# Reordering the first two groups of the MLP's up product, its passage to the down product, and the last norm

## The chip, the cores and the metric

One NeuronCore of a Trainium2 chip runs the whole program; the other seven are idle. The metric is the device time of one execution in microseconds, the median of three runs. The engines are named as in the profile: PE is TensorE (matrix products), PEld its weight loads, DVE is VectorE, ACT is ScalarE, POOL is GpSimd, SP is SyncE, which issues most DMAs. Each engine works through its own list of instructions in order; semaphores tie the lists together.

## The reference, cut to what matters

The network has two layers. Each has a norm, an attention with four groups of heads, and a squared-ReLU MLP; a norm over the result ends it. The change touches the MLP of both layers and the last norm.

```python
def rms_norm(x, g):
    xf = x.astype(jnp.float32)
    y = xf * lax.rsqrt(jnp.mean(xf * xf, axis=-1, keepdims=True) + EPS)
    return (y * g.astype(jnp.float32)).astype(x.dtype)
...
        x = x + mix @ w_out[l]
        h = rms_norm(x, norm2_g[l])
        x = x + jnp.square(jax.nn.relu(h @ w_up[l])) @ w_down[l]
    return rms_norm(x, final_norm_g)
```

There are 1024 tokens of width 1024, the MLP is 4096 wide, and all is float32.

## The kernel before

**Layout.** The activations lie transposed: eight tiles `self.x[m]` of 128 features by 1024 tokens. A float32 product is made of three passes (L219, L220, L221): an operand is split into a rounded part `hi` and a remainder `lo`, and hi·hi, hi·lo and lo·hi are added up in PSUM. A split (`split`, L187 and L193) is one ACT instruction for `hi` and one subtraction for `lo`; for weights (`weight_parts`) the subtraction is on POOL, for activations on DVE. One `block` is the product of a 512x128 piece of weights with 512 tokens: 12 PE instructions of 512 columns.

**The up product** (`mlp_up`) treats weights and activations as 2x2 blocks and makes seven products per group instead of eight. A group `q` of 16 is 128 features of each half of the MLP's width. Its seven blocks are `p12`, `p11`, `p6`, `p5`, `p7`, `p4`, `p3`. They use sums and differences of the four weight pieces (`combos`, tiles `raw`) and seven operands `ops[1]` to `ops[7]`, which are made once per layer out of `x` (tiles `oph`/`opl`, `far`, with the intermediates `t` and `v`). PSUM has two banks each for `u`, `p`, `q`, `mm`. `p11`, `p6`, `p7` and `p4` of one group run into the same bank `u`, and between them ACT copies the state out (L1237, L1247, L1256). The results meet on DVE: the copy of `p7` plus `p5` gives `s.u3` (the addition in `done4`), `p3` and the copy of `p6` give `s.u2`.

The norm is not applied to the operands. Its factor is found beside the products (`sums`, tile `acc`; `rstd_cols`, L266 on PE, L268, L246 to L256) and spread over the partitions by PE (`spread_here`, L302) into `self.rb`. It is multiplied in when a result passes the ReLU (`relu2`, L1220, followed by the square on ACT, L1222). So the first results wait for `rb`. The groups 0 and 1 (`first`) run side by side product by product, because their operands are being made meanwhile; from group 2 on a group runs on its own and the p4 and p3 of the group before come in its middle.

**The passage.** The results go to DRAM (`acts`, L1226) and come back as operands `act` of the down product, which is split into `far` tiles again. `mlp_down` uses the same seven products, in four rounds `j`; all eight PSUM banks are its own. The loads and splits of its first round are called early (high priority, offset `AHEAD`).

**What sets the order.** In the MLP, PE runs in the order in which the code is written (`manual_schedule`). The other engines' lists are laid out by a scheduler that simulates the program and takes the earliest ready instruction. After that every list is fixed. Buffers come from pools: ten `raw` pieces, nine `ev` pieces, three pairs of split weights `wh`/`wl` (a split for a block can start when the block three places before it is done), sixteen wide tiles that hold `far`, `acc`, `t`, `v`.

**The last norm.** `final(n)` works on 512 of the 1024 tokens: for each of eight tiles a square (L1455) and a scaling (L1456) on ACT and an addition on DVE, then `rstd_cols`, a spread on PE, a copy to `self.rb` on DVE (L1465), and per tile one product on DVE and one store. `final(0)` stands ahead of the last four blocks of the down product, `final(1)` behind them.

## Time and profile before

| what | us |
|---|---|
| median of three runs | 2698.26 (2697.42 to 2702.37) |
| the profiled execution | 2701.14 |
| its span, first to last instruction | 2698.9 |
| attention of layer 1 and of layer 2 | 6.8 to 697.9, 1343.4 to 2031.3 |
| up product, layer 1 and 2, begin | 698, 2031 |
| down product, layer 1 and 2, begin | 1037, 2369 |
| PE idle, gaps over 0.2 us in the timeline added up, 640 to 800 | 14.1 |
| the same, 1960 to 2698.9 | 26.8 |

Rows of a timeline give the start, the duration, engine, line, operation, and what is written from what; in brackets stands the idle time of that engine just before and who ended it. Rows of windows give for a stretch its length, the busy time of each engine with the number of instructions (x), the granted clock of TensorE as a share, the share of the DMA engines and their GB/s. PE instructions overlap: one of 512 columns is shown with 0.39 us and more, and the next one starts 0.23 us after it.

### The profile page before, as it was taken

Reading aid. Unit: us, or ns where it says so; the run is one execution under the profiler, and the core shown is the slowest. Engines: PE = TensorE matmul, PEld = TensorE weight load, DVE = VectorE, ACT = ScalarE, POOL = GpSimd, SP = SyncE. Lnnn points to the kernel's source line nnn. Section 1 sums busy time; section 2 is a strip of 40 time slices with the busy share of each in tenths; the row PEclk is TensorE's granted clock in tenths of the full one; section 3 lists DMA queues with packets and bytes.
Section 4 is the critical chain, followed back from the end, with each engine's and each line's share of the span. In section 5 each row is a group of like instructions: output and inputs, shape, how many; then the busy total and the mean of one; then the engine's idle time right before and its main releaser. Section 6 shows DMA issues by size and latency. Waiting matters only on the chain.

```text
span 2698.9 us, 37585 instructions
## 1 busy us (share of the span) xinstructions
PE 2545.4 (94%) x12296; PEld 2109.5 (78%) x12296; DVE 1944.6 (72%) x3368; ACT 1438.1 (53%) x2591; POOL 1151.6 (43%) x816
## 2 busy tenths in 40 slices
PE   8999988999889999999999999789998999999997
PEld 6778876787778887888877788677886788778886
DVE  6777767784966669887568776577749666687776
ACT  4677756663534444444437776566635344444444
POOL 2555633301345554544425655332013455545552
PEclk9989998999999999999999899899999999999998
DMA  5534597421144457444245436963221444664431
GB/s 171 174 94 141 151 268 245 106 89 57 53 140 153 150 166 269 149 139 142 100 128 149 119 114 192 273 199 89 71 71 55 156 150 151 230 219 150 131 102 63
DMA packets 191666, 389.18 MB, mean 144 GB/s; under 512 B 23840, under 2 KB 33008, under 8 KB 191472
## 3 DMA queue, kind: packets, MB, share of 16 engines
q1 hardware_dynamic: 177648, 361.62, 43.3%
q10 hardware_dynamic: 13824, 25.17, 2.7%
q8 instruction: 97, 1.59, 0.2%
q14 instruction: 97, 0.79, 0.1%
HBM read 263.29 MB, written 123.41 MB: 143 GB/s over the span
## 4 chain that ended last, share of the span: by engine, by line
PE 73%; DVE 13%; DMA 5%; ACT 5%; issue 3%; POOL 1%; SPq 0%; DVEq 0%; ACTq 0%; POOLq 0%
PE u L219 8%; PE u L221 8%; PE u L220 8%; PE mm L219 6%; PE mm L220 5%; PE mm L221 5%; PE p L219 5%; PE p L220 5%; PE p L221 5%; PE sb L815 3%; DVE p L817 2%; DVE part L187 2%; PE tr L851 2%; ACT p L820 2%; DVE ptl L187 1%
## 5 line engine op out<-in xcount | busy, mean ns | idle before, releaser
L187 POOL TENSOR_TENSOR wl<-raw,wh 128x512 fp32r<-128x512 f32 x448 | 636.0, 1420 | 699.0 <-ACT wh L193 680.1
L193 ACT ACTIVATE wh<-raw 128x512 fp32r<-128x512 f32 x448 | 281.6, 629 | 575.0 <-PE u L220 314.6
L187 POOL TENSOR_TENSOR wl<-ws,wh 128x512 fp32r<-128x512 f32 (+1 forms) x120 | 151.2, 1262 | 431.2 <-ACT wh L193 427.1
L219 PE MATMUL u<-far,wh 128*128 128x512 f32 x768 | 301.5, 393 | 12.6 <-ACT ev L1247 8.3
L187 DVE TENSOR_TENSOR ptl<-tr,pth 128x512 fp32r<-128x512 f32 (+2 forms) x384 | 239.2, 629 | 88.4 <-ACT pth L193 87.2
L221 PE MATMUL u<-far,wl 128*128 128x512 f32 x768 | 300.8, 392 | 0.8 <-POOL wl L187 0.8
L187 DVE TENSOR_TENSOR raw<-raw 128x512 f32<-128x512 f32 x256 | 222.7, 875 | 107.9 <-POOL wl L187 54.2
L220 PE MATMUL u<-far,wh 128*128 128x512 f32 x768 | 300.5, 391 | 0.0
L193 ACT ACTIVATE pth<-tr 128x512 fp32r<-128x512 f32 (+2 forms) x384 | 206.2, 547 | 123.1 <-PE tr L851 67.2
L820 ACT ACTIVATE p<-p,nm 128x1024 f32<-128x1024 f32 x192 | 220.2, 1147 | 77.3 <-DVE nm L817 72.8
L219 PE MATMUL p<-far,wh 128*128 128x512 f32 x640 | 252.3, 394 | 7.5 <-DVE ev L187 7.5
L221 PE MATMUL p<-far,wl 128*128 128x512 f32 x640 | 251.0, 392 | 1.5 <-POOL wl L187 1.5
L220 PE MATMUL p<-far,wh 128*128 128x512 f32 x640 | 251.2, 392 | 0.0
L815 PE MATMUL sb<-stack 96*128 96x512 f32 x640 | 217.6, 422 | 13.1 <-DVE nm L817 12.8
L187 DVE TENSOR_TENSOR far<-act,far 128x512 fp32r<-128x512 f32 x224 | 210.4, 969 | 14.6 <-ACT far L193 14.6
L187 POOL TENSOR_TENSOR p<-p 128x1024 f32<-128x1024 f32 x64 | 153.5, 2402 | 110.8 <-ACT p L903 103.0
L219 PEld LDWEIGHTS u<-far,wh 128*128 128x128 f32 x768 | 145.4, 189 | 45.2 <-ACT ev L1247 9.2
L851 PE MATMUL tr<-ident,p 128*128 128x128 f32 x1024 | 163.2, 278 | 8.8 <-DVE ptl L187 6.0
L221 PEld LDWEIGHTS u<-far,wl 128*128 128x128 f32 x768 | 145.1, 189 | 32.2 <-POOL wl L187 1.6
L219 PE MATMUL mm<-xh,wh 128*128 128x512 f32 x416 | 168.3, 405 | 1.4 <-DVE part L187 1.2
L220 PEld LDWEIGHTS u<-far,wh 128*128 128x128 f32 x768 | 145.3, 189 | 30.1
L220 PE MATMUL mm<-xl,wh 128*128 128x512 f32 x416 | 165.3, 397 | 0.0
(248 smaller groups left out, 6110.1 us busy)
## 6 DMA issues: line engine op xcount, KB each, us to landing
act<-acts SPq DMA_DIRECT2D x224, 256.0 KB
raw<-in_w_up SPq DMA_DIRECT2D x128, 256.0 KB
acts<-ev SPq DMA_DIRECT2D x128, 256.0 KB
raw<-in_w_down SPq DMA_DIRECT2D x128, 256.0 KB
acts<-ev ACTq DMA_DIRECT2D x96, 256.0 KB
ws<-in_w_in SPq DMA_DIRECT2D x76, 256.0 KB
rz<-drows SPq DMA_DIRECT2D x40, 256.0 KB
stack<-kd SPq DMA_DIRECT2D x32, 256.0 KB
```

The lines of the kernel that those rows point to most:

```text
L187: (eng or self.nc.vector).tensor_tensor(out=out, in0=a, in1=b, op=op)
L193: nc.scalar.activation(hi, src, AF.Copy)
L219: mm(ps, w[0], x[0][:, sl], start=start, stop=False)
L220: mm(ps, w[0], x[1][:, sl], start=False, stop=False)
L221: mm(ps, w[1], x[0][:, sl], start=False, stop=stop)
L815: self.nc.tensor.matmul(ps, q[:, qt * P:(qt + 1) * P], k[:, sl], start=i == 0, stop=i == len(passes) - 1)
L817: self.nc.vector.tensor_tensor_reduce(out=p[:, sl], in0=ps, in1=self.zero[:, 0:1].bitcast(F).broadcast_to([P, 512]), scale=-scale, scalar= ...
L820: self.nc.scalar.activation(p, p, AF.Exp, bias=nm[:, 1:2], scale=-1.0, accum_out=z)
L851: nc.tensor.transpose(t[:, k * 256 + i * P:k * 256 + (i + 1) * P], p[:, (j * 2 + k) * P:(j * 2 + k + 1) * P], self.ident)
```

## The change

It has four parts.

1. The `lo` parts of the weights of groups 0 and 1 (12 per layer) are made on DVE instead of POOL (`self.lows`).
2. At the norm's sum: the addition of `s.u3` moves from `done4` into `p4`, ahead of its block; `p4` of both first groups stands ahead of `rstd_cols`; `p12` of group 2 stands between `rstd_cols` and `spread_here`; and the rest of groups 0, 1 and 2 is interleaved instead of in sequence.
3. At the passage the first splits (`lo` on DVE), products and loads of the down product are queued on DVE behind the last group's addition `s.sum` (`issue_after`).
4. The last norm works on pieces of 512, 256 and 256 tokens, as three generators which are advanced between the last products. The last two weight blocks are split once and multiplied in halves of 256 tokens (`products`, `tail`). The spread factor is read from PSUM by DVE and from a copy of it by POOL, which makes every third of the output products.

```diff
     def weight_parts(self, raw):
...
-        self.split(wh, wl, raw, eng=self.nc.gpsimd)
+        self.split(wh, wl, raw, eng=self.lows)
...
             def p4(s):
+                s.sum = self.tt(s.u3, s.p, s.u3, ALU.add)
                 self.block(s.u, s.c["22"], ops[4], start=False)
...
                 keep(s.q, 2, s.b21)
-                self.tt(s.u3, s.p, s.u3, ALU.add)
                 relu2(s.u3, s.u3, 1)
...
                 first = [group(q) for q in range(2)]
+            self.lows = nc.vector
...
             acc = sums(1, (4, 5, 6, 7, 0, 1, 2, 3), acc)
-            p4(first[0])
+            for s in first:
+                p4(s)
             r = self.rstd_cols(acc, DM, self.ones[:, 0:1])
-            p4(first[1])
+            self.lows = nc.gpsimd
+            s = group(2)
+            p12(s)
             self.spread_here(rb, r)
-            for s in first:
-                done11(s)
-                done4(s)
+            done11(first[0])
+            done4(first[0])
             ops[3] = [self.rows_split(far(), x(k + 4, 1), gk(k + 4)) for k in range(4)]
-            for s in first:
-                p3(s)
-            held = []
-            for q in range(2, 16):
+            p3(first[0])
+            p11(s)
+            done11(first[1])
+            done4(first[1])
+            combos(s.c)
+            p3(first[1])
+            done11(s)
+            p6(s)
+            p5(s)
+            p7(s)
+            held = s
+            for q in range(3, 16):
...
+            self.settled = s.sum
...
-                b = [self.rows_split(self.far(), v) for v in t]
-                for m in M:
-                    self.block(u[m], a11[m], b)
-                    add(m, 0, u[m])
-                a12, b = [w(m, 1, "b") for m in M], op(2)
+                with ExitStack() as behind:
+                    if j == 0:
+                        behind.enter_context(tc.issue_after(self.settled.ins))
+                    b = [self.rows_split(self.far(), v) for v in t]
+                    for m in M:
+                        self.block(u[m], a11[m], b)
+                        add(m, 0, u[m])
+                    a12, b = [w(m, 1, "b") for m in M], op(2)
...
-                if last and j == 3:
-                    self.final(0)
-                for m in M:
+                if not (last and j == 3):
+                    for m in M:
+                        self.block(p[m], a12[m], b, start=False)
+                        add(m, 1, p[m])
+                    continue
+                fin = [self.final(slice(i * 256, i * 256 + w)) for i, w in ((0, 512), (2, 256), (3, 256))]
+                for f in fin:
+                    for m in (4, 5, 6, 7):
+                        next(f)
+                    if f is fin[0]:
+                        for m in M:
+                            next(f)
+                def tail(m, ws, i, f):
+                    sl = slice(i * 256, i * 256 + 256)
+                    self.products(p[m][:, sl], ws, [(h[:, sl], v[:, sl]) for h, v in b])
+                    o = self.x[m][:, 512 + i * 256:512 + i * 256 + 256]
+                    self.tt(o, p[m][:, sl], o, ALU.add)
+                    next(f)
+
+                for m in (0, 1):
                     self.block(p[m], a12[m], b, start=False)
                     add(m, 1, p[m])
-            if last:
-                self.final(1)
+                    for f in fin[1:]:
+                        next(f)
+                    if m == 0:
+                        next(fin[0])
+                ws = [self.weight_parts(a12[m]) for m in (2, 3)]
+                tail(2, ws[0], 0, fin[1])
+                next(fin[0], None)
+                tail(3, ws[1], 0, fin[1])
+                tail(2, ws[0], 1, fin[2])
+                with tc.high_priority(offset=40):
+                    next(fin[1])
+                tail(3, ws[1], 1, fin[2])
...
+        near = self.piece("ev")[:, :w]
+        nc.scalar.activation(near, rb, AF.Copy)
+        yield
+        for i, (m, x) in enumerate(xs):
+            if i % 3 == 1:
+                self.tt(x, x, near, eng=nc.gpsimd)
+            else:
+                self.tt(x, rb, x)
             self.store(self.out[m][:, sl], x)
```

**How the lists stand now: first groups.** A piece of the difference of DVE's list in layer 1, where the operands of groups 0 and 1 are made (`x_7177` and its like are tiles of `x`, `t` an intermediate, `wl` the `lo` part of a weight piece).

```order
 L187 TENSOR_TENSOR acc<-acc,sq 128x512
+L187 TENSOR_TENSOR wl<-raw,wh 128x512
 L187 TENSOR_TENSOR t<-x_7177 128x512
 L187 TENSOR_TENSOR x_7184<-mm,sum 128x512
+L187 TENSOR_TENSOR wl<-raw,wh 128x512
 L187 TENSOR_TENSOR t<-x_7184 128x512
 L187 TENSOR_TENSOR x_7191<-mm,sum 128x512
+L187 TENSOR_TENSOR wl<-raw,wh 128x512
 L187 TENSOR_TENSOR t<-x_7191 128x512
```

The first three of the twelve `wl` have come into DVE's list, between the instructions that make the operands.

**The passage, DVE, before.** The rows from the last of group 14's four differences on; `act` are loaded operands of the down product, `ev_10074<-p_10057,ev_10074` is the addition that becomes `s.sum` of group 15, the `raw` rows are sums and differences of weights for the down product.

```order
L187 TENSOR_TENSOR ev_10030<-ev_10001,ev_10029 128x512
L187 TENSOR_TENSOR far_10170<-act_10162,far_10170 128x512
L187 TENSOR_TENSOR far_10173<-act_10164,far_10173 128x512
L187 TENSOR_TENSOR far_10176<-act_10166,far_10176 128x512
L187 TENSOR_TENSOR raw_10312<-raw_10278,raw_10280 128x512
L187 TENSOR_TENSOR far_10179<-act_10168,far_10179 128x512
L187 TENSOR_TENSOR far_10266<-act_10258,far_10266 128x512
L187 TENSOR_TENSOR raw_10278<-raw_10154,raw_10278 128x512
L187 TENSOR_TENSOR far_10269<-act_10260,far_10269 128x512
L187 TENSOR_TENSOR far_10272<-act_10262,far_10272 128x512
L187 TENSOR_TENSOR raw_10334<-raw_10282,raw_10284 128x512
L187 TENSOR_TENSOR ev_10074<-p_10057,ev_10074 128x512
```

And the same place of the change:

```order
L187 TENSOR_TENSOR ev_10030<-ev_10002,ev_10029 128x512
L187 TENSOR_TENSOR raw_10312<-raw_10278,raw_10280 128x512
L187 TENSOR_TENSOR raw_10278<-raw_10154,raw_10278 128x512
L187 TENSOR_TENSOR raw_10334<-raw_10282,raw_10284 128x512
L187 TENSOR_TENSOR ev_10074<-p_10057,ev_10074 128x512
L187 TENSOR_TENSOR far_10170<-act_10162,far_10170 128x512
L187 TENSOR_TENSOR far_10173<-act_10164,far_10173 128x512
L187 TENSOR_TENSOR far_10176<-act_10166,far_10176 128x512
```

Seven splits have moved from ahead of the addition to behind it; the three `raw` rows stay ahead of it.

**The passage, ACT, before.** A little later in layer 1: `wh_10233` and `wh_10295` are the `hi` parts of the weights of the down product's fourth and fifth block, and the square of `ev_10039` (L1222) waits for DVE's `relu2` of group 15's `s.u2`.

```order
L193 ACTIVATE far_10481<-act_10472 128x512
L1222 ACTIVATE ev_10039<-ev_10039 128x512
L193 ACTIVATE far_10484<-act_10474 128x512
L193 ACTIVATE wh_10233<-raw_10160 128x512
L193 ACTIVATE far_10487<-act_10476 128x512
L193 ACTIVATE wh_10295<-raw_10250 128x512
```

And of the change:

```order
L193 ACTIVATE far_10484<-act_10474 128x512
L193 ACTIVATE far_10487<-act_10476 128x512
L1222 ACTIVATE ev_10039<-ev_10039 128x512
L193 ACTIVATE wh_10233<-raw_10160 128x512
L193 ACTIVATE wh_10295<-raw_10250 128x512
```

The two splits of `act` have moved ahead of the square, and the fourth block's `hi` part stands directly behind it, as before behind the square. The attention of layer 2, which the diff does not touch, also stands in another order on all engines, since the scheduler arrives there in another state; that of layer 1 is unchanged.

More of the change, by code (lines that the diff above doesn't have):

```diff
@@ L147, in __init__ @@
         self.ctx, self.tc, self.nc, self.d, self.out = ctx, tc, tc.nc, d, out
-        self.ahead, self.tails = 4, deque()
+        self.ahead, self.tails, self.lows = 4, deque(), tc.nc.gpsimd
         pool = lambda **k: ctx.enter_context(tc.tile_pool(**k))
@@ L1453, in final @@
             x = self.x[m][:, sl]
[L1454 removed]
+            s = self.piece("ev")[:, :w]
             nc.scalar.activation(s, x, AF.Square)
@@ L1461, in final @@
             xs.append((m, x))
+            yield
         r = self.rstd_cols(acc, DM, self.ones[:, 0:1], "u")
-        rb = self.bank("u")
-        self.spread_half(rb, r, 0)
-        nc.vector.tensor_copy(self.rb[:, sl], rb)
-        for m, x in xs:
-            self.tt(x, x, self.rb[:, sl])
+        yield
+        rb = self.bank("u")[:, :w]
+        for t in range(w // P):
+            nc.tensor.matmul(rb[:, t * P:(t + 1) * P], r[:, t:t + 1].broadcast_to([P, P]), self.ident,
+                             start=True, stop=True)
+        near = self.piece("ev")[:, :w]
+        nc.scalar.activation(near, rb, AF.Copy)
+        yield
+        for i, (m, x) in enumerate(xs):
[3 more added lines that the diff above has]
+                self.tt(x, rb, x)
             self.store(self.out[m][:, sl], x)
```

25 lines of the change are left out of this document (16 added, 9 removed).

## The prediction, made before the change was run

> **What bounds the kernel now.** I read the page's busy shares first, then the windows by stage, then PE's timeline for its gaps, then the list of the engine that ends each gap.
>
> ```profile
> span 2698.9 us, 37585 instructions
> PE 2545.4 (94%) x12296; PEld 2109.5 (78%) x12296; DVE 1944.6 (72%) x3368; ACT 1438.1 (53%) x2591; POOL 1151.6 (43%) x816
> ```
>
> PE is busy 94% of the span, so a gain can only come from PE's idle time and from its halved clock. The windows say where these are.
>
> ```profile
> 6.80:697.90 691.10, 646.69 (x3412) 539.50 (x3413) 491.12 (x1090) 428.34 (x799) 261.26 (x184) 0.96 0.49 146
> 697.95:772.84 74.89, 60.99 (x249) 48.17 (x248) 64.89 (x85) 37.50 (x67) 25.71 (x17) 0.91 0.28 92
> 800.00:850.00 50.00, 50.00 (x221) 41.20 (x220) 34.11 (x40) 21.33 (x38) 25.94 (x18) 1.00 0.45 149
> 1018.30:1041.00 22.70, 17.86 (x70) 13.91 (x69) 22.66 (x29) 12.46 (x23) 7.81 (x6) 0.92 0.88 332
> 1041.00:1071.20 30.20, 28.83 (x126) 23.21 (x126) 30.20 (x36) 15.97 (x27) 18.35 (x12) 1.00 0.54 176
> 1343.40:2031.30 687.90, 641.25 (x3414) 538.16 (x3413) 488.85 (x1081) 423.38 (x793) 258.08 (x183) 0.96 0.47 140
> 2031.27:2105.21 73.94, 60.99 (x250) 47.88 (x248) 65.13 (x85) 37.85 (x67) 25.68 (x17) 0.91 0.29 93
> 2079.00:2086.00 7.00, 6.41 (x29) 5.58 (x30) 5.48 (x10) 1.38 (x3) 0.31 (x1) 0.76 0.20 75
> ```
>
> In the steady up product (800 to 850) PE never waits: 221 instructions in 50 us, 0.226 us each, so a block of 12 costs 2.71 us. The two stretches of 74 and 75 us are the first groups of each layer, up to where group 2 begins its p7. They hold 18 blocks (48.8 us) and 32 short instructions of sum and spread, by my estimate 3.6 us at full clock; the other 22.5 and 21.5 us are waiting and half clock. At the passage (1018 to 1071) DVE is busy without a hole, 22.66 of 22.70 and 30.20 of 30.20 us: DVE, not PE, sets the pace there. PE's gaps:
>
> ```profile
> 728.26 0.50 PE L219 MATMUL u<-far,wh 128*128 128x512 f32 x1 [4.14 <-ACT ev L1247]
> 746.12 0.38 PE L302 MATMUL mm<-ident,rs_r 128*128 128x128 f32 x1 [3.26 <-DVE rs_r L256]
> 764.54 0.80 PE L219 MATMUL u<-oph,wh 128*128 128x512 f32 x1 [3.84 <-ACT ev L1237]
> 1032.25 0.50 PE L219 MATMUL p<-far,wh 128*128 128x512 f32 x1 [3.75 <-DVE ev L187]
> 1045.85 0.50 PE L221 MATMUL u<-far,wl 128*128 128x512 f32 x1 [0.34 <-POOL wl L187]
> 1071.23 0.47 PE L219 MATMUL u<-far,wh 128*128 128x512 f32 x1 [1.06 <-ACT far L193]
> 2079.59 2.48 PE L302 MATMUL mm<-ident,rs_r 128*128 128x128 f32 x16 [2.29 <-DVE rs_r L256]
> 2684.69 0.49 PE L266 MATMUL u<-ones,ev 128*128 128x1 f32 x3 [2.70 <-DVE ev L187]
> ```
>
> A gap costs more than its length. Around the 2.29 us gap at 2079.59 the granted clock over 7 us is 0.76, so 0.24 x 7.00 x 2 = 3.4 us ran at half speed, and 1.7 us of work were lost. I take 1.7 us per new gap of 2 us and more, as this row has it.
>
> **The first groups: lows on DVE.** What a POOL low costs DVE stands in these rows.
>
> ```profile
> 712.25 0.67 DVE L187 TENSOR_TENSOR opl<-t,oph 128x512 fp32r<-128x512 f32 x1
> 712.94 1.73 POOL L187 TENSOR_TENSOR wl<-raw,wh 128x512 fp32r<-128x512 f32 x1 [3.09 <-DVE opl L187]
> 713.46 1.76 DVE L1292 SCALAR_TENSOR_TENSOR t<-x,par,t 128x512 f32<-128x512 f32 x1
> 715.14 0.68 DVE L187 TENSOR_TENSOR far<-v,far 128x512 fp32r<-128x512 f32 x1
> 715.74 0.74 DVE L1292 SCALAR_TENSOR_TENSOR v<-x,par,v 128x512 f32<-128x512 f32 x1
> L187 POOL TENSOR_TENSOR wl<-raw,wh 128x512 fp32r<-128x512 f32 x12 | 17.6, 1473 | 45.1 <-ACT wh L193 40.2 <-DVE opl L187 3.1 <-DVE v L1292 1.8
> ```
>
> The DVE instruction that meets a POOL low takes 1.76 instead of 0.74 us: 1.02 to 1.07 us of DVE per low. On DVE itself a low should cost 0.60 us (0.68 less the overlap with the next, as the starts 715.14 and 715.74 show). So 12 lows moved save DVE 12 x (1.05 - 0.60) = 5 us, and each arrives within 0.7 us instead of 1.47. Bounds: no relief at all, 12 x 0.60 = 7.2 us more on DVE; or every one relieved, and none late.
>
> I followed DVE's new list by count, 0.60 us an addition and 0.66 us a three-operand one, from the end of this addition without its stretch (691.2):
>
> ```profile
> 690.60 1.76 DVE L187 TENSOR_TENSOR acc<-acc,sq 128x512 f32<-128x512 f32 x1
> 695.43 0.69 DVE L187 TENSOR_TENSOR x<-mm,sum 128x512 f32<-128x512 f32 x1 [1.14 <-PE mm L221]
> 737.13 1.47 DVE L187 TENSOR_TENSOR acc<-acc,sq 128x512 f32<-128x512 f32 x2
> 742.63 0.15 DVE L268 TENSOR_SCALAR ms<-mm 128x8 f32<-128x8 f32 x1
> 743.97 1.22 DVE L254 SCALAR_TENSOR_TENSOR rs_t<-rs_r 128x8 f32<-128x8 f32 x1
> 745.90 0.17 DVE L256 SCALAR_TENSOR_TENSOR rs_r<-rs_t,rs_r 128x8 f32<-128x8 f32 x1
> ```
>
> The low of p5 of group 0 is the 32nd instruction (26 x 0.60 + 6 x 0.66 + about 1.2 of waiting for PE, as at 695.43): 712.0. PE wants it at 697.95 + 4 x 2.71 + 0.6 + 2 x 0.226 = 709.9, so PE waits 2.2 us there, 0.6 at p11, and 1.0 at p7 for the last `far<-v`. PE is through both p4 at 697.95 + 12 x 2.71 + 3.8 = 734.3. The sum's last addition is the 68th (56 x 0.60 + 12 x 0.66 + 1.2, and three POOL lows of later blocks, 3.2): 737.1, against 738.6 now. So PE waits for the sum instead, about 2.8 us less 0.9 for the half that is ready. So DVE stays the bound of this stretch; the gain is that p4 of group 1 is done ahead of the sum.
>
> **The norm's sum.** From the last addition: 0.9 us of sum on PE, two operand lows on DVE (1.3), then the chain from `ms` to `rs_r`, 746.07 - 742.63 = 3.44 us now with a stretched step of 1.22, about 3.1 then. The spread starts at 737.1 + 0.9 + 0.5 + 3.2 = 741.7 instead of 746.12, 4.4 us earlier, and p12 of group 2 (2.71) has run under the wait: PE is 7.1 us ahead. The wait of 3.84 us ahead of p6 of group 2, whose copy stands behind eight differences, shrinks to about 1.1, since three differences and one group's squares stand ahead of it now: 9.8 us. The clock at half after 764.54 goes too (about 2.5); against it I book a wait of 2 us at p7 of group 2 (its copy is behind the second group's late squares) and one new half clock, 1.7. Layer 1: **8.6 us**. Layer 2 loses 1 us less now (73.94 against 74.89): **7.6 us**. Bounds for each: 3 (no relief on DVE) to 14 (only the waits that the order forces).
>
> By the Trainium skill (TensorE: Matmul & The Clock Gate, Part 1: The HAM clock gate) half clock follows an idle window of about 3.4 us, so waits of 2 us would cost no clock. The trace shows otherwise (2.29 us, clock 0.76). By the page the sum would be 3.4 us better.
>
> **The passage.** The order shows the addition ahead of seven splits, so the 3.75 us wait at 1032.25 goes and p3 follows p4. What is late next?
>
> ```profile
> 1031.52 0.68 DVE L187 TENSOR_TENSOR ev<-p,ev 128x512 f32<-128x512 f32 x1
> 1040.35 0.68 DVE L1220 SCALAR_TENSOR_TENSOR ev<-ev,rb 128x512 f32<-128x512 f32 x1
> 1041.07 0.63 ACT L1222 ACTIVATE ev<-ev 128x512 f32<-128x512 f32 x1
> 1042.13 0.62 ACT L193 ACTIVATE wh<-raw 128x512 fp32r<-128x512 f32 x1
> ```
>
> The `hi` part of the down product's fourth block (1042.13) stands on ACT behind the square of group 15's `u2` (1041.07), and this behind DVE's `relu2` at 1040.35. In the new list 27 DVE instructions stand between group 14's last difference and that `relu2`, 24 before: it ends about 1.8 us later, at 1042.9, and the fourth block's weights are ready at 1046, as now (1045.85). PE, ahead by 5 us after p3, waits there instead, in one piece, and loses a clock window. DVE's work up to the addition that frees the bank for 1071.23 is the same 58 instructions. So the 3.75 us are not won: I book **-1.5 us** per layer (1.7 of clock, some of it in the 1.06 us of slack). Bounds: +6.5 (3.75, its half clock 1.7 and 1.06 all go) to -3.4 (two windows). If DVE's cover were gone, that is if it had free time here, the upper bound would hold.
>
> **The last norm.**
>
> ```profile
> 2665.56 1.35 POOL L187 TENSOR_TENSOR wl<-raw,wh 128x512 fp32r<-128x512 f32 x1 [0.32 <-ACT wh L193]
> 2665.71 0.68 DVE L187 TENSOR_TENSOR x<-p,x 128x512 f32<-128x512 f32 x1
> 2690.29 4.90 DVE L187 TENSOR_TENSOR x<-x,rb 128x512 f32<-128x512 f32 x8
> 2672.11 23.45 SPq L162 DMA_DIRECT2D out<-x  x16
> ```
>
> Now 34 us pass from the end of the p5 blocks (2664.9) to 2698.9. Then: two blocks and the sum (6.3) to 2671.2, a half block, the spread and a half block (3.7) to 2674.9. Five output products of 0.65 us stand on DVE ahead of the next additions: 2678.5; square, addition and sum: 2679.2; the last half block to 2680.5; addition, square, addition, sum, five products of the middle piece and the chain of `rs_r`: 2685.3; spread, copy and five narrow products: 2687.7. Its stores land 3.7 us later, as now (2690.29 + 4.90 = 2695.2, span end 2698.9): 2691.4, a gain of **7.5 us**. Bounds: 11 (DVE never in the way) to 4 (clock halved in the half blocks, POOL's products last).
>
> The DVE products read PSUM; such a row beside a POOL low keeps its 0.68 us (2665.71), so I charge POOL's nine products nothing. The Trainium skill (SBUF — State Buffer, Who interferes with whom) says this too: only a DVE instruction with two SBUF inputs meets POOL's reads. Charged like the others, they would take 9 x 1.05 = 9.5 us off, and the gain of this part would be gone.
>
> **The second attention** gets another order. The same work takes 691.10 and 687.90 us in two orders now; I take 0, with -5 to +5.
>
> **Sum.** 8.6 + 7.6 - 3.0 + 7.5 = 20.7 us. The profiled execution (span 2698.9, 2701.14 in all) would become 2680.4; it lies 2.9 us above the median, and from the median 2698.26 comes 2677.6. I say **2677 us**.
>
> **Rivals.**
> - *The passage pays.* If DVE is quicker there than my count, each layer wins 6.5 instead of -1.5: 16 us more, 2661. For it: the addition is ahead of the splits. Against: DVE's two full windows. 0.22.
> - *No relief on DVE in the first groups*: 3 us a layer instead of 8, 2687. For it: DVE is full there already. Against: the 0.67 beside the 1.76. 0.15.
> - *Slower.* A low on DVE costs the stretched 1.75 us instead of 0.60, with ACT and PE at the same tiles: 12 x 1.15 = 13.8 us more per layer on DVE, 27.6, and 2705. It decides from about 1.5 us per low. Against it: nothing of POOL runs there any more. 0.05.
> - *No change.* The parts work but the second attention's new order takes them back: 20 of 688 us, 3%. 0.06.
>
> My forecast holds with 0.52 (2668 to 2686). A measurement of this kernel tells 0.2%, 5.4 us, from no change. Faster: 0.52 + 0.22 + 0.15 = 0.89; same 0.06; slower 0.05. The range 2657 to 2690 takes in both faster rivals and leaves out about 0.15.
>
> **What would show it.** In the new trace: no DVE instruction of 1.7 us between 692 and 730; the spread of layer 1 at 741 to 743; p3 of group 15 directly behind p4, then a wait of 4 to 7 us in the fourth block of the down product, ended by ACT `wh` or POOL `wl` at about 1046 less what is won ahead; the last PE instruction about 2685 on the old scale. I am wrong if the fourth block does not wait, or if lows on DVE take over 1 us.

## The result and the profile after

The changed kernel takes **2683.99 us** (median of five runs, 2680.68 to 2689.33), against 2702.37 us (2697.42 to 2707.92) for the kernel before on the same chip: a ratio of 0.9935, 95% interval 0.9915 to 0.9955. Timed once more beside other kernels it took 2684.57 us, ratio 0.9954 (0.9936 to 0.9972). So it is faster by about half a per cent, 12 to 18 us. The prediction said 2677 us, 20.7 us less than before by its sum; the two profiled executions differ by 14.2 us (spans of 2698.9 and 2684.7).

The head of the page of the changed kernel:

```profile
span 2684.7 us, 37657 instructions
PE 2545.3 (95%) x12320; PEld 2113.1 (79%) x12320; DVE 1932.0 (72%) x3402; ACT 1443.0 (54%) x2612; POOL 1121.1 (42%) x801
```

PE is busy as long as before (2545.3 against 2545.4 us): nothing was taken from its work, only from its idle time. The windows of the changed kernel, first groups of both layers, the steady up product, DVE's passage, and the norm's sum with p12 of group 2:

```profile
697.70:766.95 69.25, 60.65 (x250) 48.72 (x248) 61.32 (x93) 37.73 (x67) 11.56 (x8) 0.90 0.29 92
2024.91:2093.80 68.89, 59.99 (x250) 48.12 (x249) 61.23 (x93) 37.85 (x67) 11.44 (x8) 0.90 0.30 98
800.00:850.00 50.00, 50.00 (x221) 41.24 (x220) 34.07 (x40) 20.72 (x37) 26.52 (x19) 1.00 0.46 152
1020.88:1052.00 31.12, 25.22 (x96) 19.73 (x95) 31.12 (x42) 13.31 (x23) 12.05 (x7) 0.89 0.71 249
738.97:745.60 6.63, 6.63 (x21) 5.47 (x22) 4.29 (x10) 1.99 (x5) 0.00 (x0) 0.54 0.00 0
```

The first groups, 74.89 and 73.94 us before, take 69.25 and 68.89. In the fourth row DVE still works without a hole, 31.12 of 31.12 us. The last row is a price: PE runs at 0.54 of its clock over the sum and p12 of group 2. PE's gaps in the timeline of the changed kernel:

```profile
711.93 0.56 PE L221 MATMUL p<-far,wl 128*128 128x512 f32 x1 [1.94 <-DVE wl L187]
738.97 1.37 PE L266 MATMUL mm<-ones,acc 128*128 128x1 f32 x8 [2.33 <-DVE acc L187]
759.72 0.56 PE L219 MATMUL u<-oph,wh 128*128 128x512 f32 x1 [3.67 <-ACT ev L1237]
1031.73 0.47 PE L219 MATMUL u<-far,wh 128*128 128x512 f32 x1 [3.69 <-DVE ev L1220]
1041.79 0.50 PE L221 MATMUL u<-far,wl 128*128 128x512 f32 x1 [2.22 <-POOL wl L187]
2668.15 1.01 PE L266 MATMUL u<-ones,ev 128*128 128x1 f32 x4 [2.22 <-DVE ev L187]
2676.25 1.19 PE L1519 MATMUL u<-ident,rs_r 128*128 128x128 f32 x4 [1.82 <-DVE rs_r L256]
```

Gone are the 4.14 us ahead of p4 of group 0 and the 3.26 us ahead of the spread. Still there is the wait ahead of p6 of group 2 (3.67, 3.84 before). At the passage the 3.75 us ahead of p3 of group 15 are gone, and 3.69 us stand ahead of the second block of the down product.

For a balance I cut both executions at the same pieces of work, by the start times in PE's timeline: first groups (p12 of group 0 to p12 of group 3), steady groups (to p6 of group 15), passage (to the sixth operand's round), rest of the down product (to the next attention; in layer 2 to the end of the fourth operand's round), last norm.

| stretch, us | before | after | after, second profile |
|---|---|---|---|
| attention 1 / 2 | 698.0 / 687.9 | 697.7 / 685.3 | 695.0 / 688.1 |
| first groups, layer 1 / 2 | 77.6 / 76.7 | 72.0 / 71.6 | 70.4 / 71.8 |
| steady groups, each layer | 240.4 | 240.4 | 240.4 |
| passage, layer 1 / 2 | 43.2 / 43.1 | 46.6 / 45.2 | 46.6 / 45.0 |
| rest of the down product, 1 / 2 | 284.2 / 262.5 | 282.9 / 261.1 | 282.9 / 261.1 |
| last norm | 45.0 | 41.5 | 41.2 |

After less before: -0.3 and -2.6 for the attentions, -5.6 and -5.1 for the first groups, +2.1 and +0.8 for passage and rest together, -3.5 for the last norm: -14.2 us, the difference of the spans.

### The profile page after: what moved, and what is told of

It is laid out like the page before. It is cut to its first block, busy times and chain, and to the rows that moved or that the text cites. A ratio compares the mean times of both kernels' runs of the same rounds, so it can differ in the third digit from the quotient of the medians.

```text
span 2684.7 us, 37657 instructions
## 1 busy us (share of the span) xinstructions
PE 2545.3 (95%) x12320; PEld 2113.1 (79%) x12320; DVE 1932.0 (72%) x3402; ACT 1443.0 (54%) x2612; POOL 1121.1 (42%) x801
## 4 chain that ended last, share of the span: by engine, by line
PE 72%; DVE 12%; DMA 6%; ACT 5%; issue 3%; POOL 1%; SPq 0%; POOLq 0%; DVEq 0%; ACTq 0%
PE u L219 8%; PE u L221 8%; PE u L220 8%; PE mm L219 6%; PE mm L220 5%; PE mm L221 5%; PE p L221 5%; PE p L219 5%; PE p L220 5%; PE sb L815 3%; DVE p L817 3%; PE tr L851 2%; DVE part L187 2%; ACT p L820 2%; DVE ptl L187 2%
## 5 line engine op out<-in xcount | busy, mean ns | idle before, releaser
L187 POOL TENSOR_TENSOR wl<-raw,wh 128x512 fp32r<-128x512 f32 x424 | 596.9, 1408 | 725.2 <-ACT wh L193 566.7
L820 ACT ACTIVATE p<-p,nm 128x1024 f32<-128x1024 f32 x192 | 220.2, 1147 | 75.2 <-DVE nm L817 71.5
L221 PE MATMUL p<-far,wl 128*128 128x512 f32 (+1 forms) x648 | 253.0, 390 | 3.9 <-DVE wl L187 3.9
L219 PE MATMUL p<-far,wh 128*128 128x512 f32 (+1 forms) x648 | 253.9, 392 | 0.0
L220 PE MATMUL p<-far,wh 128*128 128x512 f32 (+1 forms) x648 | 252.9, 390 | 0.0
L187 DVE TENSOR_TENSOR far<-act,far 128x512 fp32r<-128x512 f32 x224 | 204.6, 945 | 15.3 <-ACT far L193 15.3
L219 PEld LDWEIGHTS u<-far,wh 128*128 128x128 f32 x768 | 145.3, 189 | 41.7 <-ACT far L193 8.4
```

The source lines that it names most:

```text
L187: return (eng or self.nc.vector).tensor_tensor(out=out, in0=a, in1=b, op=op)
L219: mm(ps, w[0], x[0][:, sl], start=start, stop=False)
L220: mm(ps, w[0], x[1][:, sl], start=False, stop=False)
L221: mm(ps, w[1], x[0][:, sl], start=False, stop=stop)
L820: self.nc.scalar.activation(p, p, AF.Exp, bias=nm[:, 1:2], scale=-1.0, accum_out=z)
```

## The experiments

The kernels ran in four lots, each beside the kernel before on its own chip. One thing is needed to read the times: attention 1 is the same program in all of them, but for its last few instructions, and took from 691.9 us (`norm_only`) to 700.1 (`ev_in_place`). So a time can be off by several us for reasons that lie outside the change, and the stretches tell more. They are told for layer 1 / layer 2. They vary too: in layer 1 the first groups of the kernel before and of `norm_only`, whose lists agree there instruction by instruction, take 77.6 and 76.4 us; those of the changed kernel, of its second profile, of `no_passage` and of `down_deferred`, which also agree, take 72.0, 70.4, 70.0 and 70.4. A difference of 2 us in the first groups can be chance.

### Part 1 alone, and the change without it

`lows_only` is the kernel before, with `weight_parts` reading `self.lows` as in the change, and with

```diff
                 first = [group(q) for q in range(2)]
+            self.lows = nc.vector
...
             p4(first[1])
+            self.lows = nc.gpsimd
```

> The kernel before with part 1 alone (lo parts of the weights of groups 0 and 1 on DVE). The stretch from p12 of group 0 to p12 of group 3 takes 77.6 us (layer 1) and 76.7 (layer 2) before, 72.0 and 71.6 in the changed kernel. Theory A: the subtractions of POOL stretch DVE's, DVE sets the pace, so part 1 alone brings the norm's sum forward: no stretched addition of 1.7 us between 692 and 725, PE's gap of 4.14 us ahead of p4 of group 0 falls under 1 us, and the stretch is 3 to 5 us shorter in each layer; time 6 to 10 us below the kernel before. Theory B: the relief is nothing because DVE takes over the work itself, and all of the 5.6 and 5.1 us come from the new order around the sum: the stretch stays within 1 us of 77.6 and 76.7, time within 2 us of before.

Measured: 2693.12 us, ratio 0.9973 (0.9960 to 0.9985). First groups 75.3 / 75.2, so 2.3 and 1.5 us less: less than A, more than B. Against `norm_only` (76.4 / 76.5) it is 1.1 and 1.3. The time is 6.8 us under that of the kernel before, as A has it, but 3.5 us of that may be the second attention's (684.4 us in this profile). The timeline of `lows_only` shows where the relief went:

```profile
737.49 1.87 PE L266 MATMUL mm<-ones,acc 128*128 128x1 f32 x8 [4.57 <-DVE acc L187]
761.33 0.79 PE L219 MATMUL u<-oph,wh 128*128 128x512 f32 x1 [4.88 <-ACT ev L1237]
```

The 4.14 us ahead of p4 are gone, but PE then waits 4.57 us for the sum: this comes 40.8 us after the start of p12 of group 0 (737.49 less 696.68), and in the kernel before its last addition ended 40.7 us after it (738.60 less 697.95). **Part 1 did not bring the sum forward at all.**

`lows_on_pool` is the changed kernel without `self.lows = nc.vector`.

> The changed kernel without part 1: all lo parts of weights on POOL, the new order around the norm's sum stays. From p12 of group 0 to p12 of group 3 the kernel before takes 77.6 and 76.7 us, part 1 alone 75.3 and 75.2, the changed kernel 72.0 and 71.6. Theory A: the two parts add up, part 1 being worth about 2 us a layer: 73.5 to 74.5 us in each layer and about 4 us more time than the changed kernel. Theory B: part 1 is needed for the new order to pay, because without it p4 of both groups is not done ahead of the sum: 75.5 us or more. Theory C: part 1 is worth nothing beside the new order: 71.5 to 72.5.

Measured: 2689.73 us, ratio 0.9974 (0.9958 to 0.9989); the changed kernel beside it 0.9954. First groups 72.4 / 73.6, against 72.0 / 71.6 and 70.4 / 71.8 with part 1: 0.4 to 2.0 us (by the first profile C in layer 1, A in layer 2; with the 70.0 of `no_passage` 2.4). B falls: the new order alone is worth 5.2 and 3.1 us (4.0 and 2.9 against `norm_only`), though p4 comes late. In layer 1 PE waits the same 4.14 us ahead of p4 as before,

```profile
726.03 0.80 PE L219 MATMUL u<-far,wh 128*128 128x512 f32 x1 [4.14 <-ACT ev L1247]
```

but then not at the sum, and p12 of group 2 fills the wait for the spread. Most of the gain in the first groups belongs to part 2.

### Three more low parts on DVE

```diff
-            self.lows = nc.gpsimd
             s = group(2)
             p12(s)
...
             p11(s)
+            self.lows = nc.gpsimd
```

> The changed kernel, where the lo parts of three more blocks (p12 and p11 of group 2, p3 of group 0) are made on DVE too. In the changed kernel three POOL subtractions at 731.7, 734.9 and 737.0 lie on the last six additions of the norm's sum, which take 7.4 us instead of 3.7; PE then waits 2.33 us and runs 6.8 us at half clock. Theory A: each costs DVE 1.2 us and would cost 0.6 on DVE itself, so the sum is ready 1 to 2 us earlier, the wait falls under 1.5 us, the half clock over p12 of group 2 goes, and the spread starts 3 to 5 us earlier; the stretch from p12 of group 0 to p12 of group 3 falls from 72.0 to 67 to 70, time 3 to 8 us under the changed kernel's. Theory B: the wait of 3.7 us ahead of p6 of group 2 is set by something that does not depend on the spread, and takes back what is won: the stretch stays at 71 to 73.

Measured: 2683.82 us, ratio 0.9937 (0.9923 to 0.9950). First groups 67.7 / 67.2: 4.3 and 4.4 us less than in the changed kernel's first profile (2.7 and 4.6 less than in its second; 2.3 to 4.3 in layer 1 over the four profiles of one order), as A says; B falls. The time does not show A's 3 to 8 us (ratio 0.9937 against 0.9935 and 0.9954); in this profile the second attention took 692.8 us (685.3 and 688.1 in the changed kernel). What the three POOL subtractions did in the changed kernel is seen in its timelines of POOL and DVE:

```profile
730.99 2.58 DVE L187 TENSOR_TENSOR acc<-acc,sq 128x512 f32<-128x512 f32 x2
731.73 1.29 POOL L187 TENSOR_TENSOR wl<-raw,wh 128x512 fp32r<-128x512 f32 x1 [59.55 <-DVE acc L187]
734.09 4.82 DVE L187 TENSOR_TENSOR acc<-acc,sq 128x512 f32<-128x512 f32 x4
734.89 1.81 POOL L187 TENSOR_TENSOR wl<-raw,wh 128x512 fp32r<-128x512 f32 x1 [1.87 <-DVE acc L187]
736.97 1.40 POOL L187 TENSOR_TENSOR wl<-raw,wh 128x512 fp32r<-128x512 f32 x1 [0.27 <-ACT wh L193]
```

Six additions take 7.40 us beside three POOL subtractions. In `lows_three` PE waits only 1.04 us for the sum (timeline), and p12 of group 2 behind it runs at full clock (windows):

```profile
734.07 1.05 PE L266 MATMUL mm<-ones,acc 128*128 128x1 f32 x8 [1.04 <-DVE acc L187]
```

```profile
734.07:738.40 4.33, 3.92 (x20) 3.06 (x20) 4.26 (x10) 2.47 (x5) 0.00 (x0) 1.00 0.00 0
```

Sum and p12 take 4.4 us here up to the spread (734.07 to 738.48), 6.5 in the changed kernel (738.97 to 745.47). DVE's whole way to the end of the sum, from the same addition on, in windows of before, of the changed kernel, and of `lows_three`:

```profile
691.20:738.60 47.40, 40.60 (x168) 31.50 (x167) 44.94 (x57) 28.85 (x51) 17.60 (x13) 0.96 0.14 39
```

```profile
690.95:738.90 47.95, 43.09 (x183) 34.41 (x181) 45.29 (x70) 30.42 (x53) 4.50 (x3) 0.96 0.16 44
```

```profile
688.74:734.00 45.26, 41.40 (x183) 33.24 (x181) 43.88 (x73) 30.35 (x53) 0.00 (x0) 1.00 0.16 47
```

The third and fifth numbers in brackets are the instructions of DVE and of POOL. Without any POOL subtraction DVE works 43.88 us on 73 instructions, 15 of them lows at 0.60 us. Without these, and without the one addition that the kernel before does not have there (0.60), that is 34.3 us for the 57 of before, which took 44.94: 13 POOL subtractions cost 10.7 us, 0.82 each. In the changed kernel 45.29 less 12 x 0.60 less 34.9 (58 instructions) leaves 3.2 us for three, 1.07 each. So DVE pays 7.2 us for its own lows and 0.6 for the addition, and is relieved of 10.7 less 3.2: it ends the sum with 0.3 us more work than before.

### The differences in place

The four differences in `p3` need three new `ev` buffers. Here they go into the buffers of `p1`, `u3` and `b21`:

```diff
-                t1, t2, n4 = tmp(), tmp(), tmp()
-                sub(t1, s.u2, s.p1)
+                sub(s.p1, s.u2, s.p1)
...
-                sub(t2, s.u3, t1)
                 sub(s.u2, s.u3, s.u2)
+                sub(s.u3, s.u3, s.p1)
...
-                sub(n4, s.b21, t2)
+                sub(s.b21, s.b21, s.u3)
```

> The changed kernel, where the four differences of a group are written in place (no new ev buffers; two of them in another order). The copy of p11 of group 2 then finds a free ev buffer instead of one that is read last by the third difference of group 0 on DVE. Theory A: the wait of 3.67 and 3.92 us ahead of p6 of group 2 is for that buffer: it goes or falls under 1 us, with its half clock (1.7), and the stretch from p12 of group 0 to p12 of group 3 falls from 72.0 and 71.6 to 66 to 69; time 5 to 10 us under the changed kernel's if the second attention keeps its length (685 us). Theory B: DVE is behind by that much anyway, and the wait appears again at p7 or at p12 of group 3: 71 to 72 us.

Measured: 2681.49 us, ratio 0.9942 (0.9924 to 0.9960). First groups 64.9 / 65.3, 7.1 and 6.3 us less than in the first profile of the changed kernel (5.5 and 6.5 less than in the second): A, and a little more. The time is 3.1 us under the changed kernel's beside it, less than A's 5 to 10; the second attention took 689.6 us, more than A's condition allows. In the changed kernel the copy of p11 waits for the third difference (the second row is ACT's, in one timeline with DVE's):

```profile
755.61 3.43 DVE L187 TENSOR_TENSOR ev<-ev 128x512 f32<-128x512 f32 x3 [0.70 <-ACT ev L1222]
759.07 0.60 ACT L1237 ACTIVATE ev<-u 128x512 f32<-128x512 f32 x1 [2.52 <-DVE ev L187]
```

In `ev_in_place` there is no wait ahead of p6, and of B's kind only this one at p7:

```profile
762.15 0.50 PE L219 MATMUL u<-far,wh 128*128 128x512 f32 x1 [1.29 <-ACT ev L1247]
```

But the passage grew to 49.3 / 47.7 us: with every group in place, the last ones pay 2.7 and 2.5 us that the first ones had won. So the wait at p6 was for a buffer, not for DVE as such.

### The passage

`no_passage` is the changed kernel without this line:

```diff
-                        behind.enter_context(tc.issue_after(self.settled.ins))
```

> The changed kernel without part 3: nothing of the down product is queued behind the last group's addition. From p6 of group 15 to the round of the down product's sixth operand the kernel before takes 43.2 and 43.1 us, the changed one 46.6 and 45.2; what follows in the down product is 1.3 us shorter in the changed one. Theory A: DVE sets the pace of the passage, so the wait only moves: without part 3 the wait of 3.7 us stands ahead of p3 of group 15 again, the one of 3.7 us ahead of the second block of the down product goes, and the two stretches are at 43 us again; the time is 0 to 4 us under the changed kernel's. Theory B: part 3 is a gain whose price is paid elsewhere: 3 to 8 us slower than the changed kernel.

Measured: 2689.35 us, ratio 0.9962 (0.9946 to 0.9977). In its timeline the wait is back ahead of p3, and the fourth block waits too:

```profile
1023.10 0.50 PE L219 MATMUL p<-far,wh 128*128 128x512 f32 x1 [3.75 <-DVE ev L187]
1038.53 0.50 PE L221 MATMUL u<-far,wl 128*128 128x512 f32 x1 [2.16 <-POOL wl L187]
```

Passage and rest together: 327.9 / 305.4, against 329.5 / 306.3 with part 3 and 327.4 / 305.6 before. That spoke for A, in part: up to the sixth operand it is 45.0 / 43.0 us, and A had 43 for both. The time is above the changed kernel's, against A, but the second attention took 697.3 us in this profile. I took that for chance and asked again, below.

`down_deferred` moves other work of DVE's out of the way:

```diff
                     s1.append(self.raw_weights("b"))
-                    self.tt(s1[m], a21[m], a22[m], ALU.add)
-                    sub(a21[m], a11[m], a21[m])
-                    sub(a11[m], s1[m], a11[m])
+                    with ExitStack() as later:
+                        if j == 0:
+                            later.enter_context(tc.issue_after(self.opened.ins))
+                        self.tt(s1[m], a21[m], a22[m], ALU.add)
+                        sub(a21[m], a11[m], a21[m])
+                        sub(a11[m], s1[m], a11[m])
```

(`opened` is the last of the four additions of the first operand's blocks.)

> The changed kernel, where the twelve weight sums and differences of the down product's first round wait on DVE for the addition that ends its first operand's blocks, instead of running as soon as their loads have landed. Theory A: DVE's load at the passage sets its length, and these instructions (7 us of DVE, none needed before the sixth operand) are in the way: the wait of 3.7 us ahead of the second block and that of 2.2 us in the fourth fall under 2 us together, and the stretch from p6 of group 15 to the sixth operand's round falls from 46.6 and 45.2 us to 40 to 43, with nothing lost behind it. Theory B: they are only moved, and what waits is then the sixth operand's round: 44 us and more up to there, or as much lost behind it.

Measured: 2687.98 us, ratio 0.9961 (0.9947 to 0.9975). The passage falls to 41.7 / 42.0, and the rest grows to 287.8 / 266.1, 5 us more: together 329.6 / 308.1. That is B. Its timeline and its windows:

```profile
1048.89 0.50 PE L219 MATMUL u<-far,wh 128*128 128x512 f32 x1 [1.99 <-ACT wh L193]
1051.69 0.79 PE L221 MATMUL u<-far,wl 128*128 128x512 f32 x1 [2.06 <-POOL wl L187]
```

```profile
1016.65:1053.00 36.35, 30.15 (x125) 23.71 (x126) 36.35 (x50) 16.70 (x30) 17.30 (x10) 0.96 0.69 247
```

DVE is busy 36.35 of 36.35 us here too. Three orders of the same work, and PE waits at p3, at the second block, or at the sixth operand's round.

### The last norm alone

`norm_only` is the kernel before with part 4.

> The kernel before with part 4 alone (last norm in pieces of 512, 256 and 256 tokens). From the end of the last op(4) block to the end of the span the kernel before takes 45.0 us, the changed one 41.5. Theory A: the part is independent of the others and worth what the changed kernel shows: 41 to 42 us there and 3 to 4 us off the time. Theory B: it is worth the predicted 7.5 us and lost some of it in the changed kernel to the other parts, by the order in which the work arrives: 37 to 39 us there, 6 to 8 us off the time.

Measured: 2693.42 us, ratio 0.9979 (0.9970 to 0.9989). The last norm takes 39.8 us, 5.2 less than before: between A and B. The windows of before, of `norm_only`, and of the changed kernel:

```profile
2653.90:2698.90 45.00, 28.80 (x129) 24.13 (x127) 29.90 (x47) 19.73 (x36) 8.76 (x6) 0.81 0.25 93
```

```profile
2646.11:2685.90 39.79, 27.09 (x153) 23.50 (x151) 26.23 (x57) 23.16 (x57) 15.86 (x15) 0.89 0.30 106
```

```profile
2643.24:2684.70 41.46, 29.51 (x153) 25.82 (x151) 26.24 (x57) 23.24 (x57) 15.87 (x15) 0.80 0.29 102
```

The same 57 instructions of DVE and 15 of POOL take 39.8 or 41.5 us. The granted clock differs, 0.89 and 0.80: (0.89 - 0.80) x 41 is 3.7 us of full clock, and PE is on the path for part of it. The other parts are not the cause: `no_passage` and `ev_in_place`, which have parts 1 and 2 as well and the same lists in this stretch, also take 39.8 us, at 0.89. Twelve profiles with part 4 take 39.8 to 41.5 us, two without it 45.0 and 44.3 (`lows_only`). So part 4 is worth 3.5 to 5.2 us, as the clock falls, and neither A nor B has the reason.

### The changed kernel once more

> The changed kernel once more, as it is: shows what its own profile repeats. Every theory expects the stretches of the MLP within 0.3 us of its first profile (72.0 and 71.6; 46.6 and 45.2). For the second attention, 685.3 us in the first profile, theory A (its length hangs on the order that each kernel's scheduler gave it): 683 to 688; theory B (it varies by 10 us from run to run in one and the same order): anything up to 697.

Measured: 2684.57 us, ratio 0.9954 (0.9936 to 0.9972). The passage repeats (46.6 / 45.0), the first groups of layer 1 do not: 70.4 / 71.8 against 72.0 / 71.6, where at most 0.3 us was expected. The second attention took 688.1 us instead of 685.3, at the edge of A's span: 2.8 us in one and the same order, less than B's ten. One repeat does not exclude B: attention 1 took 698.0 us in the kernel before and 691.9 in `norm_only`, with the same lists. The 1.6 us of the first groups are clock: the same gap of 2 us ahead of p5 halved the clock in one profile of the changed kernel and not in others (last section).

### The two edits together

`both_with_passage` is the changed kernel with the three low parts of `lows_three`, and with the differences in place for `s.q < 2` alone. `both_no_passage` leaves part 3 out as well. `both_two_queues` is the latter with every second store of the last piece issued by ACT (`nc.scalar.dma_start`).

> The changed kernel with the three further lo parts on DVE and with the differences in place for groups 0 and 1 alone; part 3 stays. Three further lo parts alone gave 67.7 and 67.2 us from p12 of group 0 to p12 of group 3, differences in place for all groups 64.9 and 65.3 (and 2.6 us more at the passage). Theory A: the two waits are of one chain but each has a price of its own, so the gains add up: 60 to 63 us; passage 45 to 47 us, as in the changed kernel, since the last groups are written as there; time 10 to 14 us under the changed kernel's. Theory B: both edits remove the same time, and DVE stays behind: 64 to 66 us, time 5 to 8 us under the changed kernel's.

> The same without part 3 (nothing of the down product is queued behind the last group's addition). Theory A, part 3 costs 2 us a layer: from p6 of group 15 to the sixth operand 43 to 45 us and nothing lost behind it, time 3 to 5 us under that of the same kernel with part 3, about 2665 to 2670. Theory B, part 3 is worth something once the first groups are quick: equal or slower.

> The same without part 3, and half of the eight stores of the last piece are issued by ACT instead of SP. In the changed kernel the last product ends at 2680.04 and the span at 2684.7, 4.66 us later, 3.7 in the kernel before; SP issues its 24 stores until 2682.1. Theory A: SP's issuing in sequence sets the end, so it is 1 to 2 us earlier: 3 to 3.7 us from the last product to the end. Theory B: the transfers themselves do (they run at 250 to 290 GB/s there): 4.3 us and more.

| kernel | median, us | ratio | first groups | passage and rest | last norm |
|---|---|---|---|---|---|
| `both_with_passage` | 2674.73 | 0.9894 (0.9876 to 0.9911) | 64.1 / 63.1 | 327.9 / 308.5 | 41.5 |
| `both_no_passage` | 2670.54 | 0.9885 (0.9871 to 0.9900) | 66.0 / 62.2 | 328.8 / 306.9 | 40.9 |
| `both_two_queues` | 2674.18 | 0.9900 (0.9883 to 0.9918) | 65.5 / 63.1 | 329.6 / 306.1 | 40.8 |

By their ratios to the kernel before, all three are faster than the changed kernel, and they cannot be told apart from each other. The edits add up in part: 62 to 66 us, where 60 to 63 would be the whole and 64 to 66 one alone. The time of `both_no_passage` is 4.2 us under that of `both_with_passage`, as A of `both_no_passage` has it, but up to the sixth operand it takes 45.9 / 45.8 us, and A had 43 to 45, so A falls. Passage and rest overlap: three kernels without part 3 have 327.9 to 329.6 / 305.4 to 306.9; five profiles with part 3 and the passage as in the changed kernel 327.9 to 330.6 / 306.1 to 308.5 (`lows_on_pool` has 330.6 / 307.7). The means are 0.7 and 0.8 us apart, less than the kernels of one kind differ among themselves: a price of part 3 is neither shown nor excluded. The two queues end 4.0 us behind the last product instead of 4.6, neither A nor B, and the time shows nothing of it.

One more kernel, `sum_in_done4`, asked whether the place of the addition (`p4` instead of `done4`) makes the passage longer. It is `both_no_passage` with

```diff
             def p4(s):
-                s.sum = self.tt(s.u3, s.p, s.u3, ALU.add)
+                if s.q < 2:
+                    s.sum = self.tt(s.u3, s.p, s.u3, ALU.add)
...
                 keep(s.q, 2, s.b21)
+                if s.q >= 2:
+                    s.sum = self.tt(s.u3, s.p, s.u3, ALU.add)
```

> The kernel with both edits in the first groups and without part 3, where from group 2 on the addition to u3 also stands in done4 again, behind relu2 of b21, as in the kernel before: the passage is written wholly as before. From p6 of group 15 to the end of the fourth operand's round the kernel before takes 327.4 us in layer 1 and 305.6 in layer 2; with the addition in p4 it was 327.9 to 329.6 and 305.4 to 306.9 without part 3 (three kernels), 327.9 to 329.8 and 306.1 to 308.5 with it (four profiles). Theory A: it is the place of the addition that lengthens the passage, whether part 3 is there or not: 327.4 and 305.6 again, within 0.2. Theory B: DVE is full there and only the order in which its scheduler was led, and where the clock falls, decide: 328 and more in one layer at least.

Measured: 2673.53 us, ratio 0.9898 (0.9882 to 0.9915). Passage and rest 328.6 / 307.6: A falls; `norm_only` and `lows_only`, whose passage is written as before, repeat its 327.4 / 305.6 within 0.1 us. Its timeline has the waits of `no_passage`:

```profile
1021.62 0.79 PE L219 MATMUL p<-far,wh 128*128 128x512 f32 x1 [3.78 <-DVE ev L187]
1037.72 0.50 PE L221 MATMUL u<-far,wl 128*128 128x512 f32 x1 [1.77 <-POOL wl L187]
```

The kernel before waits 0.34 us in that fourth block. The passage's code is that of before now, but DVE and ACT got another order for it. What the fourth block waits for is one subtraction on POOL, here in `sum_in_done4` and in the kernel before:

```profile
1033.44 4.23 POOL L187 TENSOR_TENSOR wl<-raw,wh 128x512 fp32r<-128x512 f32 x1 [4.66 <-ACT wh L193]
1042.82 2.98 POOL L187 TENSOR_TENSOR wl<-raw,wh 128x512 fp32r<-128x512 f32 x1 [4.14 <-ACT wh L193]
```

It takes 1.25 us longer in the new order (4.23 us in `no_passage` too), beside a DVE that is busy for 3.71 of these 4.23 us. Why it takes longer there stays open.

## Why the prediction was right, and where its sizes were off

Of the 20.7 us booked the spans show 14.2: 5.5 less in the first groups, 4.0 less in the last norm, 0.1 more at the passage, and 2.9 us in the attentions, for which nothing was booked. The four parts alone gave 11.3 us. The time lies 2 us inside the end of the forecast's 2668 to 2686, so that it lies inside is in part luck.

**First groups and sum: 8.6 and 7.6 us booked, 5.6 and 5.1 measured** (7.2 and 4.9 in the second profile). Some of the signs that were named are there: no DVE instruction of 1.7 us between 692 and 730, lows of 0.68 us on DVE, gaps of 0.46 and 1.94 us at p11 and p5 for 0.6 and 2.2 predicted. Others are not: p7 waits 0.21 us instead of 1.0, and the spread of layer 1, named for 741 to 743, began at 745.47. Three terms were mis-sized.

- "The sum's last addition is the 68th ... 737.1": it ended at 738.9. I took 12 x 1.05 us of stretch away and put 3.2 back, 9.4 net; the windows show 10.7 less 3.2, 7.5 net. The price of 1.05 was read from the neighbours of one POOL subtraction; over 13 of them it is 0.82. With 7.8 us more of its own work DVE gained nothing.
- "One new half clock, 1.7": the clock was halved over the sum and p12 of group 2, 6.63 us at 0.54, which costs 3. The factor was ready at 743.43 and the spread began at 745.47, when PE had crept through p12 (rows of the changed kernel's timeline behind this list).
- The wait ahead of p6 of group 2 "shrinks to about 1.1": it stayed at 3.67 and 3.92. I had the third difference ahead of the copy, but not that POOL's subtractions stretch the three of them to 3.43 us. So its half clock, of which 2.5 us were booked as won, stayed for the most part: p6 and p5 of group 2 take 7.2 us (759.72 to 766.95), 8.3 before and 5.4 at full clock. The 2 us booked at p7 did not come. `ev_in_place` shows that the copy waits for the buffer.

```profile
743.26 0.17 DVE L256 SCALAR_TENSOR_TENSOR rs_r<-rs_t,rs_r 128x8 f32<-128x8 f32 x1
745.47 2.38 PE L302 MATMUL mm<-ident,rs_r 128*128 128x128 f32 x16
```

The other rival, "no relief on DVE", was nearer to the truth in its mechanism than my forecast: DVE was not relieved, and the gain came from the order around the sum. It priced the two together at 3 us a layer, and `lows_on_pool` shows 5.2 and 3.1 for the order alone.

**Passage: -1.5 per layer booked, -2.1 and -0.8 measured.** This was the step that mattered for the choice between 2677 and 2661, and it held: DVE is full, the 3.75 us come back. p3 follows p4 directly, as named. The place was half wrong. I looked for one wait of 4 to 7 us in the fourth block; there are 3.69 us ahead of the second and 2.22 in the fourth. DVE's, ACT's and POOL's timelines of the changed kernel show why:

```profile
1021.48 7.09 DVE L187 TENSOR_TENSOR far<-act,far 128x512 fp32r<-128x512 f32 x8
1030.91 0.67 DVE L1220 SCALAR_TENSOR_TENSOR ev<-u,rb 128x512 f32<-128x512 f32 x1
1037.63 0.63 ACT L1222 ACTIVATE ev<-ev 128x512 f32<-128x512 f32 x1 [2.94 <-DVE ev L1220]
1038.17 1.65 ACT L193 ACTIVATE wh<-raw 128x512 fp32r<-128x512 f32 x3
1038.86 6.28 POOL L187 TENSOR_TENSOR wl<-raw,wh 128x512 fp32r<-128x512 f32 x3 [11.44 <-PE u L220]
```

The eight splits that part 3 queues behind the addition now stand ahead of the `relu2` that reads the `u` bank of group 15, and the down product's second block needs that bank. I had followed the `relu2` of `u2` (an SBUF tile) and not this one. The path that I had followed is there as named: the `hi` part of the fourth block stands behind the square of `u2`, and PE's wait in that block ends at 1041.79. Group 15 begins 5.87 us earlier than before, so that is 1047.7 on the old scale, for the 1046 that were named. `down_deferred` and `no_passage` show that other orders move the wait; that the rest of the cost is DVE's load as a whole is what the three full windows say, and no run took load away.

**Last norm: 7.5 booked, 5.2 alone, 3.5 in the changed kernel** (3.8 in its second profile; both lie under the lower bound of 4). The end of the changed kernel, DVE and POOL:

```profile
2663.77 3.08 DVE L187 TENSOR_TENSOR x<-u,x 128x512 f32<-128x512 f32 x5
2677.90 1.75 DVE L187 TENSOR_TENSOR x<-u,x 128x256 f32<-128x256 f32 x5 [1.79 <-ACT ev L1522]
2677.95 2.09 POOL L187 TENSOR_TENSOR x<-x,ev 128x256 f32<-128x256 f32 x3 [2.56 <-ACT ev L1522]
```

PE's last spread began at 2676.25 and took 1.19 us at half clock; both engines then begin behind the copy (2677.9), and the three POOL products end at 2680.04: 3.9 us from the chain's end (2676.11), where I had 2.4 (2685.3 to 2687.7). The stores land 4.66 us later, not 3.7. In `norm_only` the same two steps take 3.9 and 4.65 us. They make up the 2.3 us by which part 4 alone fell short. The five products at 2663.77 keep 0.60 us each beside POOL's, so I was right to charge these nothing. The Trainium skill (SBUF — State Buffer, Who interferes with whom) says so of instructions with one SBUF input, and the trace agrees.

**Second attention: 0 booked, with 5 either way; 2.6 less in one profile, 0.1 more in the other.** Right for this kernel, and its spread (684.4 to 697.3 us over all profiles) is most of what blurs the times above.

What is shown by a run: the price of a POOL subtraction beside DVE, the buffer ahead of p6, the cost of the three POOL subtractions at the sum, the range of part 4's own gain. What is only read from the traces: that DVE's load sets the passage. What stays open: whether part 3 has a price, which order at the passage gives the 327.4 us of the kernel before, and how much of the attention's spread is chance.

## What to carry to other kernels

Where an engine is full, an edit that takes a wait away from another engine may only give it a new place, as three orders did here: count the instructions of the full engine up to the next thing that is wanted of it, PSUM banks included, and take work off it rather than reorder it. Moving work between two engines that slow each other pays only where the last of the disturbing instructions goes too: the twelve moved subtractions gave DVE nothing, and three that stayed cost the first groups 2 to 4 us. And a wait for a copy may be a wait for the copy's target: the cheapest edit of this case was to free three buffers.

## What the runs showed of the hardware

**The same gap does and does not cost the clock.** PE waits 1.94 to 1.99 us ahead of the same instruction of p5 in several kernels. The windows of the 3.4 us that follow, in the changed kernel and in `lows_three`:

```profile
711.93:715.30 3.37, 3.37 (x9) 2.63 (x10) 3.37 (x6) 0.63 (x1) 0.00 (x0) 0.54 0.58 128
```

```profile
709.73:713.10 3.37, 3.37 (x15) 2.79 (x16) 3.37 (x6) 1.27 (x2) 0.00 (x0) 1.00 0.45 144
```

9 instructions and a clock of 0.54, or 15 and 1.00. The Trainium skill (TensorE: Matmul & The Clock Gate, Part 1: The HAM clock gate) calls the gate's window free-running, which fits: a gap would count differently by where it falls in the window. Its figure of about 3.4 us of idleness is longer than the gaps that halved the clock here (1.94 and 2.33 us). The traces show what decides here. In each of the fourteen, the granted clock is recorded to change only on a grid of 3.41 us, and where the grid lies differs from execution to execution. Windows along it, around the wait at p5 of the changed kernel in layer 1, in its first profile and in its second:

```profile
708.82:712.23 3.41, 1.47 (x7) 0.91 (x6) 3.41 (x6) 2.24 (x4) 0.00 (x0) 1.00 0.00 0
712.23:715.65 3.42, 3.42 (x9) 2.65 (x8) 3.42 (x7) 0.63 (x1) 0.00 (x0) 0.50 0.64 153
```

```profile
704.13:707.55 3.42, 3.01 (x12) 2.18 (x12) 3.42 (x7) 1.34 (x3) 0.00 (x0) 1.00 0.00 0
707.55:710.96 3.41, 1.75 (x8) 1.46 (x9) 3.41 (x7) 2.10 (x4) 0.00 (x0) 1.00 0.22 58
710.96:714.37 3.41, 3.41 (x17) 2.83 (x16) 3.41 (x7) 1.42 (x3) 0.00 (x0) 1.00 0.28 96
```

In the first profile the wait lies inside one window: PE is busy for 1.47 of its 3.41 us, and the next window runs at half clock. In the second profile two windows share the wait, and the clock stays. This wait occurs thirteen times in all profiles. Seven times PE was busy for 1.47 us or less of a window, and each time the next one was at half clock; six times it was busy for 1.63 us or more of every window that the wait touched, and the clock stayed. So a booked half clock is a chance, that of how the grid falls, and two profiles of one kernel differ by 1.6 us in the first groups for it.

**A program repeats unevenly.** The steady groups took 240.4 us in every profile of every kernel and both layers; attention 1, the same instructions but for its last few, took 691.9 to 700.1.
